# Newest sum first, and the next low weight parts behind the leading narrow products

## The chip, the cores and the metric

One NeuronCore of a Trainium2 chip runs the whole program. The metric is the device time in microseconds of one execution; of the kernel before, three runs were timed.

## The reference, cut to what matters

One decoder block over 256 tokens of width 2048, all in float32:

```python
x = x + 0.5 * swiglu(rms_norm(x, g1), w1_gate, w1_up, w1_down)      # 2048 -> 5632 -> 2048
z = rms_norm(x, gm) @ w_in                                           # 2048 -> 9216
# differential attention of 8 heads on q, k, v; causal depthwise convolution on the GLU part;
# both go through 1024 -> 2048 projections, are gated by sigmoids and added
x = x + merged @ w_out
x = x + 0.5 * swiglu(rms_norm(x, g2), w2_gate, w2_up, w2_down)
return rms_norm(x, final_norm_g)
```

Almost all of the work is matrix products of 256 tokens with weights that are read once from memory.

## The kernel before

**Split products.** Each float32 operand is split into a high part, the value rounded to the fp32r type that TensorE multiplies, and a low part, the remainder. A product is high times high, plus high times low, plus low times high. ScalarE (ACT) makes the high part of a weight block (`wh`, line 94), VectorE (DVE) the low part by subtraction (`wl`, line 103).

**Units and halves.** Weights come in units of 512 rows by 512 columns (1 MB, one DMA on SyncE's queue, three raw buffers). A unit has two halves of two 128-row tiles each; a half is the piece that one line-94 and one line-103 instruction split. There are six buffers for high halves and four for low halves. So the low halves of a unit can be written only when the low products of the unit two before it are done. `Weights.next` (lines 109 to 124) hands out the next half, and before that emits the splits of later halves: high ones up to six halves from the present one, low ones up to four. Behind a low part that ends a raw unit the DMA of a later unit is issued (line 107).

**`lin`** (lines 321 to 369) keeps the weights stationary and makes four PSUM tiles of 128 columns by 512: the left 256 take the high products, the right 256 the products of the low parts of the activations. Per unit there are 16 wide products (line 331, 512 moving columns: both parts of the activations against the high weights) and 16 narrow ones (line 335, 256 moving columns, low weights). Odd units and the last unit of a `lin` run narrow then wide, the others wide then narrow, so that two units' wide products, and two units' narrow ones, stand together. There are 5 PSUM buffers for such tiles, so the next `lin` takes the free one and then those of this `lin` in order. The feed-forward layers call `lin` for gate, up and the first layer's down product; the mixer for the GLU, q and k columns; and `w_out` too. `lin_tok` (lines 379 to 388) is the other form, with activations stationary.

**Carrying off.** In the last unit, after the four wide products of a column tile, that tile's evacuation generator is appended to `flows`; `tick` then takes every flow one stage further, oldest first, and runs side jobs at a given rate. A feed-forward evacuation has as its first stage ACT's copy of the right half of PSUM (line 392), DVE's sum (394) and DVE's product with the gate or the scale (424 or 404). A later stage is ACT's high part of the activation (261) and the next one DVE's low part (263); for a gate it is ACT's Silu (406) and a GpSimd product (407). `residual_evac` has two DVE sums (441, 442). Each engine runs its instructions in the order in which the program emits them.

**Start.** In the first `lin`, `before(u)` splits two tiles of x (lines 256 and 258, ACT and DVE; GpSimd squares them) one half ahead of the products, and `halves` takes the units by halves with `next(early=False)`: the low parts go four halves ahead, the high ones as they are needed.

Of the kernel before, what the change touches and what calls it, by code (L numbers as in the profile page):

```python
# [25 lines left out]
KU = 4  # L26
KH = 2
# [14 lines left out]
class Weights:  # L42
# [54 lines left out]
    def low_to(self, n):  # L97
        while self.nlow < min(n, len(self.units) * KU // KH):
# [6 lines left out]
            if k + KH == KU:  # L105
                del self.raw[u]
                self.load_to(u + 1 + self.raw_bufs)

    def next(self, held=0, early=True):


        i = self.i

        def ahead(bufs):
            n = i + bufs - held
            if self.extra and n > min(self.extra) and i <= max(self.extra):
                n = min(n + len(self.extra), max(self.extra) + 1 + bufs)
            return n

        if early:  # L120
            self.high_to(ahead(self.high_bufs))
        self.low_to(ahead(self.low_bufs))
        self.i += 1
        return self.highs.pop(i), self.lows.pop(i)

# [6 lines left out]
class Side:  # L132
# [8 lines left out]
    def tick(self, n=1):  # L141
        for job in list(self.jobs):
            job[2] += n * job[1]
            while job[2] >= 1:
                job[2] -= 1
                if next(job[0], self) is self:
                    self.jobs.remove(job)
                    break
# [7 lines left out]
def block_kernel(  # L156
# [57 lines left out]
    W = Weights(nc, wpool, units, moving)  # L214
# [97 lines left out]
    flows = []  # L312

    def tick(n=1):

        for f in list(flows):
            if next(f, flows) is flows:
                flows.remove(f)
        side.tick(n)

    def lin(nk, xs, evac, before=None):

        ps = [psum.tile([P, CK], F32, name="ps_mm", tag="mm") for _ in range(4)]
        nu = nk // KU

        def high(ct, parts, kt, i):
            w = parts[i // KH][0][:, i % KH, ct * P:(ct + 1) * P]  # L330
            nc.tensor.matmul(ps[ct], lhsT=w, rhs=xs(kt + i), start=(kt + i == 0), stop=(kt + i == nk - 1))  # L331

        def low(ct, parts, kt, i):
            w = parts[i // KH][1][:, i % KH, ct * P:(ct + 1) * P]
            nc.tensor.matmul(ps[ct][:, T:2 * T], lhsT=w, rhs=xs(kt + i)[:, 0:T], start=False, stop=False)  # L335

        def halves(u):

            for h in range(KU // KH):
                before(u * (KU // KH) + h)  # L340
                parts = [W.next(early=False)]
                for i in range(KH):
                    for ct in range(4):
                        high(ct, parts, u * KU + h * KH, i)
                for ct in range(4):
                    for i in range(KH):
                        low(ct, parts, u * KU + h * KH, i)
                tick(4)

        for u in range(nu):  # L350
            last = u == nu - 1
            if before is not None and not last:
                halves(u)
                continue
            parts = []
            for h in range(KU // KH):
                if before is not None:
                    before(u * (KU // KH) + h)
                parts.append(W.next(held=h))
            for product in ((low, high) if last or u % 2 == 1 else (high, low)):  # L360
                for ct in range(4):
                    for i in range(KU):
                        product(ct, parts, u * KU, i)
                    if product is high:
                        if last:
                            flows.append(evac(ct, ps[ct]))
                        tick(1.4)
                    elif ct % 2 == 1:
                        tick(1.2)
# [28 lines left out]
    def ffn_up(h, rstd, grp, a, before=None, late=None):  # L398
        s_2 = None

        def pair_of(ci, s_t):
# [19 lines left out]
            def up_evac(ct, ps):  # L421
# [4 lines left out]
                yield from split(a(ci * 4 + ct), t)  # L426

            lin(KT, h, gate_evac, before if ci == 0 else None)
            if late is not None and ci == 0:
                side.add(gate_late(), 0.5)  # L430
            lin(KT, h, up_evac)

        for ci in range(len(grp)):
# [14 lines left out]
    def next_norm(h, acc, g):  # L448
        def f(kt):
            yield  # L450
            add_square(acc, xT[:, kt, :], kt == 0)
            yield from split_scaled(h(kt), xT[:, kt, :], g[:, kt:kt + 1])
        return f
# [5 lines left out]
    def split_x(kt):  # L459

        fs = [split_scaled(h1(kt + k), xT[:, kt + k, :], g1_sb[:, kt + k:kt + k + 1]) for k in range(2)]
        for f in fs:
            next(f)
        for f in fs:
            next(f, None)
        for k in range(2):
            add_square(acc1, xT[:, kt + k, :], kt + k == 0, square=nc.gpsimd)

    def start(u):
        if u == 0:  # L470
            W.ahead = 1
            split_x(0)
            W.split_first()
        if u < 7:
            split_x(2 * u + 2)
        else:
            W.ahead = 3

    loads = {}

# [50 lines left out]
    for gi, grp in enumerate(groups):  # L531
        a = split_pair("Q", "a1_")
        if gi == 0:
            ffn_up(h1, rstd1, grp, a, start, rstd_steps(acc1, rstd1, D, 1e-6))
        else:
            ffn_up(h1, rstd1, grp, a)
        last = None
        if gi == len(groups) - 1:
            hm = split_pair("P", "hm_")
            accm, rstdm = norm_tiles("m")  # L540
            last = next_norm(hm, accm, loads["gm"])
        for dc in range(4):
            lin(len(grp) * 4, a, residual_evac(dc, 0.5, last))
# [487 lines left out]
```

## Time and profile before

| what | value |
|---|---|
| median of three runs | 2100.95 us (2100.57 to 2101.76) |
| profiled execution, own time | 2100.18 us |
| its span, first to last instruction | 2098.4 us |
| TensorE busy | 2065.3 us, 98% |
| VectorE busy | 1375.9 us, 66% |
| ScalarE busy | 1004.8 us, 48% |
| GpSimd busy | 190.6 us, 9% |
| mean granted TensorE clock | 0.997 |
| DMA | 189 GB/s over the span |

Busy time of an engine is the union of its instructions. TensorE's weight loads (PEld) overlap its products (PE). A row of the timeline can hold several instructions one after the other (x4), and ends with the idle time of the engine before them and what ended it.

### The profile page before, as it was taken

To read this page: it belongs to the slowest core of one execution; us is meant where nothing else is said; L and a number is where in the kernel's file an instruction comes from. 1 tells how busy PE (TensorE), PEld (TensorE's weight loads), DVE (VectorE), ACT (ScalarE), POOL (GpSimd) and SP (SyncE) were. 2 spreads that over 40 slices of the span, in tenths; PEclk is the share of its full clock that TensorE was granted. 3 is DMA by queue.
4 is the path that set the end of the run, shared out by engine and by line. 5 is a ranking of instruction groups with operands and counts; after the bars stand their busy time and mean duration, and the time that the engine had idled before them with its cause. 6 is when DMAs were issued, how large, how long until landed. Compare 5 with 4: busy or idle time off the path is not lost.

```text
span 2098.4 us, 28546 instructions
## 1 busy us (share of the span) xinstructions
PE 2065.3 (98%) x11230; PEld 1775.8 (85%) x11230; DVE 1375.9 (66%) x1915; ACT 1004.8 (48%) x1456; POOL 190.6 (9%) x227
## 2 busy tenths in 40 slices
PE   7999999999999999999999999999999999999998
PEld 6888888888888888888778888888888888888887
DVE  8565555665565785889888666665655655645565
ACT  6454344443344554445555744554443444434443
POOL 6201012110010110000000000100100001000011
PEclk9999999999999999999999999999999999999999
DMA  6645555566545545555545555554455555554553
GB/s 241 197 171 212 188 177 206 189 216 218 181 180 202 193 174 201 181 187 186 183 166 180 198 181 181 198 203 180 168 214 183 184 195 181 201 193 168 203 198 121
DMA packets 57735, 397.54 MB, mean 189 GB/s; under 512 B 6888, under 2 KB 6992, under 8 KB 10752
## 3 DMA queue, kind: packets, MB, share of 16 engines
q1 hardware_dynamic: 55872, 390.10, 52.2%
q0 software_dynamic: 1728, 5.61, 0.9%
q8 instruction: 88, 1.44, 0.3%
q14 instruction: 47, 0.39, 0.1%
HBM read 392.00 MB, written 3.68 MB: 189 GB/s over the span
## 4 chain that ended last, share of the span: by engine, by line
PE 88%; DVE 7%; ACT 2%; DMA 1%; issue 1%; SPq 0%; DVEq 0%; ACTq 0%
PE ps_mm L331 40%; PE ps_mm L335 21%; PE ps_mm L375 9%; PE ps_mm L376 9%; PE ps_mm L377 9%; DVE wl L103 3%; DVE t L394 2%; DVE t L424 1%; ACT rh L392 1%; DMA w<-in_ffn_w_gate_dram 1%; ACT a L261 1%; DMA w<-in_ffn_w_down_dram 1%; PE ps_s L718 0%; PE ps_o L763 0%; PE ps_tr L907 0%
## 5 line engine op out<-in xcount | busy, mean ns | idle before, releaser
L103 DVE TENSOR_TENSOR wl<-w,wh 128x1024 fp32r<-128x1024 f32 x731 | 883.3, 1248 | 484.2 <-ACT wh L94 239.9
L94 ACT ACTIVATE wh<-w 128x1024 fp32r<-128x1024 f32 x731 | 742.8, 1053 | 704.0 <-PE ps_mm L331 377.5
L331 PE MATMUL ps_mm<-h,wh 128*128 128x512 f32 x2816 | 665.2, 392 | 10.8 <-DVE h L258 10.8
L331 PEld LDWEIGHTS ps_mm<-h,wh 128*128 128x128 f32 x2816 | 523.0, 189 | 117.4 <-ACT wh L84 6.2
L335 PEld LDWEIGHTS ps_mm<-h,wl 128*128 128x128 f32 x2816 | 340.9, 188 | 25.4 <-DVE wl L103 18.1
L335 PE MATMUL ps_mm<-h,wl 128*128 128x256 f32 x2816 | 349.8, 279 | 11.2 <-DVE wl L103 11.2
L407 POOL TENSOR_TENSOR s_t<-s_t,rstd 128x256 f32<-128x256 f32 x88 | 82.7, 940 | 1158.8 <-ACT s_t L406 1158.8
L331 PE MATMUL ps_mm<-a,wh 128*128 128x512 f32 x704 | 164.9, 390 | 0.4 <-DVE t L394 0.4
L331 PEld LDWEIGHTS ps_mm<-a,wh 128*128 128x128 f32 x704 | 130.4, 188 | 26.9 <-DVE t L394 0.8
L392 ACT ACTIVATE rh<-ps_mm 128x256 f32<-128x256 f32 x208 | 77.3, 372 | 153.7 <-PE ps_mm L331 153.7
L375 PE MATMUL ps_mm<-wl,a 128*128 128x512 f32 (+1 forms) x344 | 133.1, 387 | 0.0
L377 PE MATMUL ps_mm<-wh,a 128*128 128x512 f32 (+1 forms) x344 | 132.1, 384 | 0.0
L376 PE MATMUL ps_mm<-wh,a 128*128 128x512 f32 (+1 forms) x344 | 131.9, 384 | 0.0
L375 PE MATMUL ps_mm<-wl,hm 128*128 128x512 f32 x320 | 129.8, 406 | 0.0
L377 PE MATMUL ps_mm<-wh,hm 128*128 128x512 f32 x320 | 125.1, 391 | 0.0
L376 PE MATMUL ps_mm<-wh,hm 128*128 128x512 f32 x320 | 124.9, 390 | 0.0
L331 PE MATMUL ps_mm<-hm,wh 128*128 128x512 f32 x512 | 121.0, 392 | 0.0
L331 PEld LDWEIGHTS ps_mm<-hm,wh 128*128 128x128 f32 x512 | 94.7, 188 | 19.1
L619 DVE SCALAR_TENSOR_TENSOR y_sb<-u_sb,cw_sb,y_sb 128x256 f32<-128x256 f32 x240 | 105.0, 478 | 0.0
L394 DVE TENSOR_TENSOR t<-ps_mm,rh 128x256 f32<-128x256 f32 x112 | 47.5, 424 | 63.1 <-ACT rh L392 62.9
L335 PEld LDWEIGHTS ps_mm<-a,wl 128*128 128x128 f32 x704 | 84.5, 188 | 4.5 <-DVE wl L103 2.7
L335 PE MATMUL ps_mm<-a,wl 128*128 128x256 f32 x704 | 85.6, 278 | 1.9 <-DVE wl L103 1.9
(194 smaller groups left out, 1708.2 us busy)
## 6 DMA issues: line engine op xcount, KB each, us to landing
w<-in_ffn_w_up_dram SPq DMA_DIRECT2D x88, 1024.0 KB, 4.9
w<-in_ffn_w_down_dram SPq DMA_DIRECT2D x88, 1024.0 KB, 4.9
w<-in_ffn_w_gate_dram SPq DMA_DIRECT2D x85, 1024.0 KB, 4.9
w<-in_w_in_dram SPq DMA_DIRECT2D x72, 1024.0 KB, 4.8
w<-in_w_out_dram SPq DMA_DIRECT2D x16, 1024.0 KB, 4.9
w<-in_w_attn_branch_dram SPq DMA_DIRECT2D x8, 1024.0 KB, 4.8
w<-in_w_conv_branch_dram SPq DMA_DIRECT2D x8, 1024.0 KB, 4.8
w<-in_ffn_w_gate_dram SPq DMA_DIRECT2D x5, 512.0 KB, 8.5
```

What stands on the lines that cost most here:

```text
L94: self.nc.scalar.activation(wh, self.raw[u][:, k:k + KH], AF.Copy)
L103: self.nc.vector.tensor_tensor(wl, self.raw[u][:, k:k + KH], self.highs[h].bitcast(F32), ALU.subtract)
L261: nc.scalar.activation(dst[:, 0:T], src, AF.Copy)
L331: nc.tensor.matmul(ps[ct], lhsT=w, rhs=xs(kt + i), start=(kt + i == 0), stop=(kt + i == nk - 1))
L335: nc.tensor.matmul(ps[ct][:, T:2 * T], lhsT=w, rhs=xs(kt + i)[:, 0:T], start=False, stop=False)
L375: nc.tensor.matmul(ps, lhsT=hi, rhs=wl[:, kk, :], start=(first and kk == 0), stop=False)
L376: nc.tensor.matmul(ps, lhsT=hi, rhs=wh[:, kk, :], start=False, stop=False)
L377: nc.tensor.matmul(ps, lhsT=lo, rhs=wh[:, kk, :], start=False, stop=(last and kk == KH - 1))
L392: nc.scalar.activation(r, ps[:, T:2 * T], AF.Copy, scale=scale)
L394: nc.vector.tensor_tensor(dst, ps[:, 0:T], r, ALU.add)
L407: nc.gpsimd.tensor_tensor(s, s, rstd, ALU.mult)
L619: nc.vector.scalar_tensor_tensor(y, src, w, y, ALU.mult, ALU.add)
```

## The change

Four edits. `tick` runs the flows newest first. `Weights.next` makes low parts up to the four-halves limit only where `early` is set; in `halves` it makes them to one half beyond the present one. A new method `more_lows(n)` emits the low parts of n halves more than `next` allows. In a unit whose narrow products lead (odd units, and the last), `more_lows(1)` is called between its narrow and its wide products, and `more_lows(2)` before the third of its four column tiles of wide products. The attribute `W.ahead`, which nothing reads, goes.

```diff
--- before.py
+++ after.py
@@ -106,6 +106,10 @@
                 del self.raw[u]
                 self.load_to(u + 1 + self.raw_bufs)
 
+    def more_lows(self, n):
+
+        self.low_to(self.i + self.low_bufs - KU // KH + n)
+
     def next(self, held=0, early=True):
 
 
@@ -119,7 +123,9 @@
 
         if early:
             self.high_to(ahead(self.high_bufs))
-        self.low_to(ahead(self.low_bufs))
+            self.low_to(ahead(self.low_bufs))
+        else:
+            self.low_to(i + 2)
         self.i += 1
         return self.highs.pop(i), self.lows.pop(i)
 
@@ -313,7 +319,8 @@
 
     def tick(n=1):
 
-        for f in list(flows):
+
+        for f in flows[::-1]:
             if next(f, flows) is flows:
                 flows.remove(f)
         side.tick(n)
@@ -357,8 +364,13 @@
                 if before is not None:
                     before(u * (KU // KH) + h)
                 parts.append(W.next(held=h))
-            for product in ((low, high) if last or u % 2 == 1 else (high, low)):
+            order = (low, high) if last or u % 2 == 1 else (high, low)
+            for product in order:
+                if product is high and order[0] is low:
+                    W.more_lows(1)
                 for ct in range(4):
+                    if product is high and order[0] is low and ct == 2:
+                        W.more_lows(2)
                     for i in range(KU):
                         product(ct, parts, u * KU, i)
                     if product is high:
@@ -468,13 +480,10 @@
 
     def start(u):
         if u == 0:
-            W.ahead = 1
             split_x(0)
             W.split_first()
         if u < 7:
             split_x(2 * u + 2)
-        else:
-            W.ahead = 3
 
     loads = {}
 
```

## Rows read from the trace of the kernel before

**Rows 1.** Page, part 1: busy us per engine, share of the span, instructions.

```profile
PE 2065.3 (98%) x11230; PEld 1775.8 (85%) x11230; DVE 1375.9 (66%) x1915; ACT 1004.8 (48%) x1456; POOL 190.6 (9%) x227
```

**Rows 2.** Waits of TensorE: who for whom, us in total, times, longest.

```profile
PE ps_mm L335 <- DVE wl L103: 13.9, 41, 0.6
PE ps_mm L331 <- DVE h L258: 10.8, 4, 5.8
...
PEld ps_mm L335 <- DVE wl L103: 22.0, 41, 0.8
```

**Rows 3.** Chain of waits in time order: start us, us, what.

```profile
68.34 7.28 PE ps_mm L331 x32
...
113.33 7.28 PE ps_mm L331 x32
...
225.28 7.28 PE ps_mm L331 x32
...
269.02 7.28 PE ps_mm L331 x32
```

**Rows 4.** Timeline, 56 to 92 us: start, us, engine, line, idle before.

```profile
57.55 0.38 ACT L392 ACTIVATE rh<-ps_mm 128x256 f32<-128x256 f32 x1 [2.14 <-PE ps_mm L331]
...
59.35 0.37 ACT L392 ACTIVATE rh<-ps_mm 128x256 f32<-128x256 f32 x1
...
62.77 0.36 ACT L392 ACTIVATE rh<-ps_mm 128x256 f32<-128x256 f32 x1
...
64.04 2.35 DVE L103 TENSOR_TENSOR wl<-w,wh 128x1024 fp32r<-128x1024 f32 x2
...
66.45 1.90 PE L335 MATMUL ps_mm<-h,wl 128*128 128x256 f32 x14 [0.51 <-DVE wl L103]
...
77.33 2.36 DVE L103 TENSOR_TENSOR wl<-w,wh 128x1024 fp32r<-128x1024 f32 x2 [5.73 <-ACT wh L94]
...
79.11 7.44 PE L331 MATMUL ps_mm<-h,wh 128*128 128x512 f32 x32
...
80.66 0.42 DVE L394 TENSOR_TENSOR s_t<-ps_mm,rh 128x256 f32<-128x256 f32 x1 [0.97 <-ACT rh L392]
```

**Rows 5.** Groups: line, engine, operation, shapes, count, busy us, mean ns, idle.

```profile
L394 DVE TENSOR_TENSOR s_t<-ps_mm,rh 128x256 f32<-128x256 f32 x88 | 37.3, 424 | 70.1 <-ACT rh L392 70.1
...
L442 DVE SCALAR_TENSOR_TENSOR xT<-ps_mm,xT 128x256 f32<-128x256 f32 x64 | 27.2, 424 | 2.2
...
L407 POOL TENSOR_TENSOR s_t<-s_t,rstd 128x256 f32<-128x256 f32 x88 | 82.7, 940 | 1158.8 <-ACT s_t L406 1158.8
```

**Rows 6.** Timeline of the start, 10 to 38 us.

```profile
13.19 1.28 DVE L103 TENSOR_TENSOR wl<-w,wh 128x1024 fp32r<-128x1024 f32 x1 [1.79 <-ACT wh L94]
...
15.04 1.78 DVE L103 TENSOR_TENSOR wl<-w,wh 128x1024 fp32r<-128x1024 f32 x1 [0.57 <-ACT wh L94]
...
16.75 1.69 DVE L258 SCALAR_TENSOR_TENSOR h<-xT,g_sb,h 128x256 fp32r<-128x256 f32 x2
...
17.63 3.78 PE L331 MATMUL ps_mm<-h,wh 128*128 128x512 f32 x8 [4.46 <-DVE h L258]
...
31.38 1.63 DVE L103 TENSOR_TENSOR wl<-w,wh 128x1024 fp32r<-128x1024 f32 x1
...
32.93 1.71 DVE L258 SCALAR_TENSOR_TENSOR h<-xT,g_sb,h 128x256 fp32r<-128x256 f32 x2
...
37.97 0.38 ACT L392 ACTIVATE rh<-ps_mm 128x256 f32<-128x256 f32 x1 [0.52 <-PE ps_mm L331]
```

**Rows 7.** Timeline around 460 us, a late weight block.

```profile
459.91 2.01 ACT L94 ACTIVATE wh<-w 128x1024 fp32r<-128x1024 f32 x2 [6.23 <-DMA w<-in_ffn_w_down_dram]
...
466.12 1.20 PE L331 MATMUL ps_mm<-a,wh 128*128 128x512 f32 x4 [0.38 <-DVE t L394]
```

**Rows 8.** Busy us per engine, clock and DMA in two 50 us windows.

```profile
1450.00:1500.00 50.00, 48.88 (x287) 42.81 (x286) 31.87 (x43) 23.29 (x35) 3.71 (x4) 1.00 0.51 185
...
1550.00:1600.00 50.00, 50.00 (x222) 41.16 (x220) 24.91 (x23) 19.67 (x19) 0.00 (x0) 1.00 0.56 197
```

## The prediction

> **What bounds the kernel now.** I read the page's busy times first. TensorE is busy 2065.3 of 2098.4 us [rows 1], so whatever the change does to the other engines counts only through some 33 us in which TensorE stands still, and through what its weight loads lose beside that. The list of waits says what ends these: 41 times the low part of a weight half (line 103), with 13.9 us of idle product time and 22.0 us of idle weight loading; and four waits on VectorE's split of x, 10.8 us in all, at the very start [rows 2].
>
> What one of the 41 costs in full is read from the chain. From the wide products at 225.28 to those at 269.02 lie eight units without such a wait: 43.74 us. From 68.34 to 113.33 lie also eight units (two linears of the gate and up columns) with two waits: 44.99 us [rows 3]. That is 0.63 us for each wait: idle time, the lost prefetch of weights and the refilling of the pipeline.
>
> The timeline shows why [rows 4]. The wait at 66.45 is in the narrow products of the second unit of a linear, and it is for the second of two low parts that VectorE began at 64.04 and made in 2.35 us. Their buffers had been free since the last unit's narrow products ended, about 1.1 us before the first copy at 57.55 (0.91 us of wide products for that tile, and 0.2 us to the copy). VectorE came so late because the program puts these two behind the four evacuations of the last unit. And these are slow: ScalarE's copies for line 392 start at 57.55, 59.35 and, the fourth, 62.77, some 1.7 us apart, while the wide products end a column tile each 0.91 us (32 of them take 7.28 us [rows 3], four to a tile). With the oldest flow first, ScalarE's next copy stands behind the older tile's split, which itself waits for VectorE's product.
>
> **Part 1, the low parts ahead of the evacuations.** I lay the new order over the linear whose wide products start at 79.11 [rows 4]. VectorE makes the next unit's pair from 77.33 to 79.69, as now. The first moved half follows to 80.87 (1.18 us, half of 2.35); its buffer came free at 79.11. The first sum, now at 80.66, starts at 80.87. A tile takes two operations of 0.42 us, with the step between them 0.9 us [rows 5]: first tile to 81.8, second to 82.7. Then the second moved half, to 83.9. The third tile's sum has read PSUM by 84.3.
>
> Two things must hold. The moved halves are needed at 79.11 + 3.64 (wide) + 3.64 (next unit, wide) + 1.83 (its narrow ones, 43.74 / 8 less 3.64) = 88.2: they are 4.3 us early, and the wait goes whole. And the next linear starts at 82.75, its fourth tile at 85.48, in the buffer that the third tile of this linear leaves at 84.3: 1.2 us to spare. `residual_evac` reads PSUM with both of its sums (0.42 us each [rows 5]), so 0.45 us later: 0.7 us to spare. In the mixer a convolution step or two stand between; I count on some margin there too. So I cost the move at nothing: the next linear's first three tiles cover it. If that cover were gone, each us of delay would be a us of TensorE.
>
> What is queued behind the new wait: the first moved half waits for the narrow products just emitted. Behind it on VectorE are the sums of tiles whose wide products come later still on TensorE, and side jobs; nothing that TensorE needs before. In odd units that are not the last there is no evacuation behind it. The moved half also frees the raw buffer earlier, so SyncE issues the next 1 MB load earlier; its queue then carries only these loads, in the same order. ScalarE's high parts are emitted six halves ahead already and don't move.
>
> Gain: 41 waits by 0.63 us, 25.6 us. From below it is bounded by the idle product time alone, 13.9 us [rows 2], if the rest were something else; I take 25.6, since the stretches differ by nothing but these waits. What is late next in these stretches: nothing that I can name; elsewhere eight-unit stretches run without a gap, and TensorE's clock is granted in full both with gaps and without (1.00 at 48.88 and at 50.00 busy of 50 us [rows 8]).
>
> **Part 2, newest flow first.** The count and length of instructions stay. A tile's sum is no longer behind an older tile's split, so sums follow the products at 0.91 us. The older stage (activation split, Silu, GpSimd product) comes one copy later, 0.4 us; its reader is a linear away, except for the last tiles before a down product, which are needed only in its last unit. Alone this would also make the low parts some 2 us earlier, so parts 1 and 2 remove the same wait twice and are counted once. One stop of its own goes: at 459.91 a weight block lands late, ScalarE stands for 6.23 us with the copies behind it, and at 466.12 a fourth tile waits for a sum, 0.38 us [rows 7]. With earlier loads and quicker sums I count 0.4 us, between 0 and 0.6.
>
> **Part 3, the start.** Now VectorE makes three low parts in a row, with 1.79 and 0.57 us of waiting for weights, and only then, at 16.75, the low part of x that TensorE waits for until 17.63, for 4.46 us [rows 6]. With low parts only one half ahead that split of x comes right behind the first of them, at some 11.4, and TensorE goes on at about 13.2, when the next weight half is ready, if x has landed. But from there VectorE is the bound: a pair of x splits (1.69 us) and a low part (1.63) take 3.3 us a half, TensorE's products 2.7. What counts is when the last unit, whose narrow products lead, has both low parts. Now all that VectorE does up to its last x split ends at 32.93 + 1.71 = 34.64. The change leaves one low part (1.63 at 31.38) for after that and fills up to 2.36 us of waiting: 30.7 to 31.3. Narrow and wide products (1.83 + 3.64) then end at 36.2 to 36.8; now they end 0.2 us before ScalarE's fourth copy, at 37.8 [rows 6]. I take 0.9 us of gain, from the later of the two. It could be 4.4 (the whole stop, if TensorE were the bound) or a loss of 1.4 (if none of VectorE's waiting is filled).
>
> The sum: 25.6 + 0.4 + 0.9 = 26.9 us from the profiled execution's own 2100.18: 2073.3. That execution was 0.8 us below the median of the three runs, so 2074.1 for a median.
>
> [...] The trace has GpSimd's products with a mean of 0.94 us, in the gate linears, beside the evacuations [rows 5], and low parts of 1.63 us in the start, where GpSimd works all the time, against 1.18 later [rows 4, 6]. [...]
>
> **The rivals.**
>
> *Half of it.* Something I don't see keeps the second moved half late, say the high half or the raw block behind which it stands. For: the waits on VectorE are for the second half of a pair. Against: high parts are two units ahead. Half of 25.6 is lost: 2087. Chance 0.06.
>
> *Blocked.* [...] Chance 0.05.
>
> *Evacuation becomes the bound, slower.* If a low part in these stretches comes to 1.63 us, the four ahead of the third sum (the pair, the first moved half, the second) push it to 84.3 + 4 x 0.45 = 86.1, and in `residual_evac` to 86.5, against 85.48. With 0.1 us to refill that is 0.7 us in each of 44 gate and up linears and 1.1 us in some 20 others: 53 us lost, 27 gained, 2127. Stops begin at a low part of 1.5 us, and from about 1.55 they outweigh the gain. Against: pairs of 2.35 us in the very stretches [rows 4]. Chance 0.04.
>
> *It doesn't do what it says*: the moved low parts wait for the same instant as before, because a low buffer is not free at 79.11. Then the order of the sums alone changes: 2100. Against: the buffer count, four, and the narrow products that end there. Chance 0.03.
>
> **How the numbers follow.** The forecast has 0.82. Its own bounds: at best 2100.18 - 25.6 - 4.4 - 0.6 + 0.8 = 2070, at worst 2100.18 - 13.9 + 1.4 + 0.8 = 2088. The range 2069 to 2087 holds nearly all of it and the edge of "half": some 0.85. A difference below 0.2%, 4.2 us, can't be told from none. Faster: forecast, half and blocked, 0.93. Same: 0.03. Slower: 0.04.
>
> **What would show it.** Right: no waits, or next to none, of line 335 on line 103; eight gate and up units in 43.7 us; VectorE's sums 0.9 us apart; in the last unit a line-103 instruction between the end of its narrow products and the first sum. At the start the stop near 17.63 gone, smaller stops later on x or low parts, and the fourth copy at 36 to 37.5. Wrong: stops of line 331 on sums (394, 442), or waits of line 335 still there at the second unit of a linear.

## The result, and the profile after

| | before | changed | ratio, 95% interval |
|---|---|---|---|
| median | 2101.34 us | 2072.3 us | 0.9862 [0.9845, 0.988] |
| range of runs | 2100.57 to 2101.76 | 2071.92 to 2072.87 | |
| span of the profiled execution | 2098.4 us | 2070.7 us | |

The forecast was 2074.1 us, in a range of 2069 to 2087. The change gains 29.0 us between the medians (27.7 between the profiled spans); 26.9 were forecast. That the totals agree so closely is in part luck: one term came out larger and another with the other sign, as the account below shows.

TensorE's row of the page, beside [rows 1]: the same products, 13.9 us less of busy time, in a span 27.7 us shorter. So about half of the gain is idle time that is gone, and half is products that took less time; the trace does not divide these further.

```profile
PE 2051.4 (99%) x11230; PEld 1771.1 (86%) x11230; DVE 1364.6 (66%) x1915; ACT 1017.2 (49%) x1456; POOL 202.1 (10%) x227
```

The list of waits, beside [rows 2] (who waited for whom, us in total, times, longest). None of the 41 waits for a low part is left: they all came after the start, and the four in the list now are new ones, all in the first 31 us. No stop on a sum has come in their place. The 6.0 us are the time until the first product; in the kernel before they are the 5.8 among the waits for x:

```profile
PE ps_mm L338 <- ACT wh L84: 6.0, 1, 6.0
PE ps_mm L342 <- DVE wl L103: 5.2, 4, 2.7
```

The chain of waits in time order, beside [rows 3]: wide products of eight units of gate and up columns. They take 43.74 us, what such units took without a wait before, where two waits made it 44.99.

```profile
68.37 7.28 PE ps_mm L338 x32
...
112.11 7.28 PE ps_mm L338 x32
```

The timeline of an up linear and the next gate linear, beside [rows 4]:

```profile
58.41 0.38 ACT L404 ACTIVATE rh<-ps_mm 128x256 f32<-128x256 f32 x1 [2.12 <-PE ps_mm L338]
...
59.32 0.38 ACT L404 ACTIVATE rh<-ps_mm 128x256 f32<-128x256 f32 x1 [0.53 <-PE ps_mm L338]
...
60.22 0.38 ACT L404 ACTIVATE rh<-ps_mm 128x256 f32<-128x256 f32 x1
...
60.64 1.22 DVE L103 TENSOR_TENSOR wl<-w,wh 128x1024 fp32r<-128x1024 f32 x1
...
61.19 0.39 ACT L404 ACTIVATE rh<-ps_mm 128x256 f32<-128x256 f32 x1
...
64.56 3.82 PE L342 MATMUL ps_mm<-h,wl 128*128 128x256 f32 x32
...
77.36 3.50 DVE L103 TENSOR_TENSOR wl<-w,wh 128x1024 fp32r<-128x1024 f32 x3 [6.36 <-ACT wh L94]
...
79.14 7.44 PE L338 MATMUL ps_mm<-h,wh 128*128 128x512 f32 x32
...
80.78 0.42 DVE L406 TENSOR_TENSOR s_t<-ps_mm,rh 128x256 f32<-128x256 f32 x1
...
82.40 1.76 DVE L103 TENSOR_TENSOR wl<-w,wh 128x1024 fp32r<-128x1024 f32 x1
...
84.09 0.41 DVE L406 TENSOR_TENSOR s_t<-ps_mm,rh 128x256 f32<-128x256 f32 x1
```

ScalarE's four copies now stand 0.9 us apart (58.41, 59.32, 60.22, 61.19), where they stood 1.7 apart. The first moved low part is the third of the three at 77.36; the first sum follows at 80.78, where the forecast had 80.87; the second moved part stands at 60.64 or 82.40, between the second and the third sum. The third sum ends at 84.5 (forecast 84.3), 1.0 us before the next linear's fourth tile needs its buffer (79.14 + 3.64 + 2.73 = 85.5). In the `w_out` linear whose wide products start at 1288.89 the same margin is 0.65 us (forecast 0.7), and in the mixer's linear at 779.96, to which the forecast gave no number, it is only 0.3 us. The narrow products at 64.56 run through 32 without a gap.

The start, beside [rows 6]:

```profile
11.14 1.72 DVE L264 SCALAR_TENSOR_TENSOR h<-xT,g_sb,h 128x256 fp32r<-128x256 f32 x2
...
13.18 2.08 PE L338 MATMUL ps_mm<-h,wh 128*128 128x512 f32 x8
...
27.46 1.69 DVE L264 SCALAR_TENSOR_TENSOR h<-xT,g_sb,h 128x256 fp32r<-128x256 f32 x2
27.59 0.50 PE L342 MATMUL ps_mm<-h,wl 128*128 128x256 f32 x2 [2.08 <-DVE wl L103]
...
29.08 6.53 DVE L103 TENSOR_TENSOR wl<-w,wh 128x1024 fp32r<-128x1024 f32 x4
...
30.76 3.36 PE L342 MATMUL ps_mm<-h,wl 128*128 128x256 f32 x14 [2.67 <-DVE wl L103]
33.92 6.68 PE L338 MATMUL ps_mm<-h,wh 128*128 128x512 f32 x24
...
38.82 0.38 ACT L404 ACTIVATE rh<-ps_mm 128x256 f32<-128x256 f32 x1 [0.52 <-PE ps_mm L338]
```

The stop near 17.63 is gone: the split of x stands at 11.14 and products go on at 13.18. But two stops have come before the last unit, 2.08 and 2.67 us, both for its low parts, and the fourth copy is at 38.82, 0.85 us later than before. The windows say why the last unit's products were slow, 14 narrow ones taking 3.36 us (columns: stretch, then busy us of TensorE, weight loads, VectorE, ScalarE and GpSimd with their counts, then granted clock, DMA share, GB/s):

```profile
28.00:30.00 2.00, 0.10 (x1) 0.00 (x0) 2.00 (x3) 0.87 (x1) 1.84 (x4) 0.83 0.17 70
30.00:32.00 2.00, 1.24 (x6) 1.24 (x7) 2.00 (x2) 1.13 (x2) 2.00 (x2) 0.50 0.35 57
32.00:34.00 2.00, 2.00 (x11) 2.00 (x11) 2.00 (x3) 0.00 (x0) 1.92 (x2) 0.50 0.79 319
34.00:36.00 2.00, 2.00 (x6) 1.57 (x6) 1.60 (x1) 0.14 (x1) 2.00 (x2) 0.50 0.79 250
```

Behind the stops the granted clock was 0.50, from about 29.3 to 36.1. Before, the only such stretch at the start lay behind the old stop:

```profile
14.00:18.00 4.00, 0.37 (x1) 0.37 (x2) 3.43 (x4) 3.92 (x7) 3.84 (x4) 0.74 1.04 425
18.00:22.00 4.00, 4.00 (x12) 3.23 (x12) 4.00 (x5) 2.03 (x4) 3.84 (x5) 0.50 1.01 428
```

### The profile page after: what moved, and what is told of

Its sections match the earlier page's. It is cut to its first block, busy times and chain, and to the rows that moved or that the text cites. A ratio compares the mean times of both kernels' runs of the same rounds, so it can differ in the third digit from the quotient of the medians.

```text
span 2070.7 us, 28562 instructions
## 1 busy us (share of the span) xinstructions
PE 2051.4 (99%) x11230; PEld 1771.1 (86%) x11230; DVE 1364.6 (66%) x1915; ACT 1017.2 (49%) x1456; POOL 202.1 (10%) x227
## 4 chain that ended last, share of the span: by engine, by line
PE 98%; DVE 0%; ACT 0%; ACTq 0%; issue 0%
PE ps_mm L338 47%; PE ps_mm L342 24%; PE ps_mm L387 9%; PE ps_mm L388 9%; PE ps_mm L389 9%; PE ps_s L727 0%; PE ps_o L772 0%; PE ps_mg L880 0%; PE ps_tr L916 0%; PE ps_at L762 0%; PE ps_mean L302 0%; PE ps_tr L815 0%; ACT sqf L976 0%; DVE x L974 0%; ACT x L995 0%; ACTq L1036 0%
## 5 line engine op out<-in xcount | busy, mean ns | idle before, releaser
L342 PE MATMUL ps_mm<-h,wl 128*128 128x256 f32 x2816 | 340.0, 278 | 5.2 <-DVE wl L103 5.2
L419 POOL TENSOR_TENSOR s_t<-s_t,rstd 128x256 f32<-128x256 f32 x88 | 89.3, 1024 | 1124.9 <-ACT s_t L418 1124.9
L389 PEld LDWEIGHTS ps_mm<-wh,a 128*128 128x128 f32 x344 | 64.5, 188 | 13.9
```

The source lines that it names most:

```text
L389: nc.tensor.matmul(ps, lhsT=lo, rhs=wh[:, kk, :], start=False, stop=(last and kk == KH - 1))
L419: nc.gpsimd.tensor_tensor(s, s, rstd, ALU.mult)
```

## The experiments

Ratios are to the kernel before, run on the same chip.

**Each part by itself.** First the moved low parts alone, in the start as before and with flows oldest first:

```diff
-        for f in flows[::-1]:
+        for f in list(flows):
...
-            self.low_to(ahead(self.low_bufs))
-        else:
-            self.low_to(i + 2)
+        self.low_to(ahead(self.low_bufs))
```

> The moved low parts alone; flows oldest first and the start as in the kernel before. Theory: each of the two order changes removes the 41 waits by itself. Then no wait of line 335 on line 103 stays, the steady part gains the 28.6 us that the changed kernel gained behind its start, and the start costs nothing: about 2072 us (2071 to 2074). Rival: the moved low parts alone push the third sum, whose copies are still 1.7 us apart, past the start of the next linear's fourth tile: stops of the wide products on sums, 2076 to 2095.

Measured: 2074.61 us, 0.9877 [0.9863, 0.989]. No wait of a narrow product on a low part is left in it, so the moved parts do remove all 41 by themselves. The time lies between the theory (up to 2074) and its rival (from 2076): it stays 2.6 us above the same kernel with newest flow first (2071.97, below), by the rival's mechanism. The timeline of a `w_out` linear shows it: oldest first, VectorE makes the second moved part (1.71 us) and then an older tile's split (line 262) before the third tile's sums, which end at 1295.42, and the next linear's fourth tile stops:

```profile
1292.04 1.71 DVE L103 TENSOR_TENSOR wl<-w,wh 128x1024 fp32r<-128x1024 f32 x1
1293.68 0.96 DVE L262 SCALAR_TENSOR_TENSOR h<-xT,g_sb,h 128x256 fp32r<-128x256 f32 x1
...
1295.00 0.42 DVE L452 SCALAR_TENSOR_TENSOR xT<-ps_mm,xT 128x256 f32<-128x256 f32 x1
...
1295.58 1.16 PE L336 MATMUL ps_mm<-mg,wh 128*128 128x512 f32 x4 [0.22 <-DVE xT L452]
```

There are three such stops, and the linears behind them fall back by 1.5 us in all against the kernel with newest flow first. The list of waits of the weight loads has five more, for first-stage sums (line 404):

```profile
PEld ps_mm L336 <- DVE t L404: 1.7, 5, 0.4
```

At these five, one of them in the up linear at 63.20, TensorE falls back by another 1.0 us in all. So nearly the whole difference is sums that came too late in the oldest-first order.

Then newest flow first alone, on the kernel before:

```diff
-        for f in list(flows):
+        for f in flows[::-1]:
```

> Newest flow first alone. Theory: copies 0.91 us apart, the fourth sum about 2 us earlier, so the pair of low parts that stands behind it is ready some 1 us before it is needed: the 41 waits go, about 2072 us (2071 to 2075). Rival: the low parts are still behind all evacuations and stay late in the linears with the longest ones: half of the waits stay, 2086; or all, 2101.

Measured: 2072.13 us, 0.9864 [0.985, 0.9877]: the whole gain from one line. The pair of low parts still stands behind all evacuations, but these are done sooner; the pair that began at 64.04 in [rows 4] begins at 62.90, though this linear is 0.7 us later (its first copy at 58.26 against 57.55), and is ready at 65.25, before the second unit's narrow products (the second half of the 32 at 64.41):

```profile
58.26 0.38 ACT L392 ACTIVATE rh<-ps_mm 128x256 f32<-128x256 f32 x1 [2.13 <-PE ps_mm L331]
...
59.17 0.38 ACT L392 ACTIVATE rh<-ps_mm 128x256 f32<-128x256 f32 x1 [0.53 <-PE ps_mm L331]
...
61.04 0.38 ACT L392 ACTIVATE rh<-ps_mm 128x256 f32<-128x256 f32 x1
...
62.90 2.35 DVE L103 TENSOR_TENSOR wl<-w,wh 128x1024 fp32r<-128x1024 f32 x2
...
64.41 3.82 PE L335 MATMUL ps_mm<-h,wl 128*128 128x256 f32 x32
```

So the two order changes remove the same waits twice, as part 2 of the prediction had it. With newest flow first in place, the moved low parts neither cost nor gain anything that can be measured: 2072.13 us without them, 2071.97 with them and the old start (next).

**The start.** Parts 1 and 2 with the start as before, and the new start alone:

```diff
-            self.low_to(ahead(self.low_bufs))
-        else:
-            self.low_to(i + 2)
+        self.low_to(ahead(self.low_bufs))
```

> The changed kernel with the low parts of the start four halves ahead as before. Theory: the new start costs 0.85 us (the second linear begins at 38.62 instead of 37.77), so 2071.5 us, 0.5 to 1.2 us below the changed kernel, second linear at 37.8. Rival: the loss in the start is given back later or was chance: 2072.3.

```diff
-        self.low_to(ahead(self.low_bufs))
+        if early:
+            self.low_to(ahead(self.low_bufs))
+        else:
+            self.low_to(i + 2)
```

> The new start alone on the kernel before. Theory: 0.85 us slower, about 2102.2 us; second linear at 38.6, and TensorE's clock granted at 0.50 behind its stop at 28 to 31 us. Rival (the prediction's own step): 0.9 us faster, 2100.4.

Measured: 2071.97 us, 0.9863 [0.9848, 0.9878], for the first, 0.3 us below the changed kernel; 2101.11 us, 1.0004 [0.9995, 1.0012], for the second, no change that can be told from none. Both medians lean towards a loss, of 0.3 and 0.8 us, but neither the theory's loss of 0.85 us nor the prediction's gain of 0.9 can be told from nothing: the new start moves the time by no more than starts differ by themselves. The product that sums the squares of x (line 296 before the change) stands at the same place of TensorE's queue in all these kernels, behind the first linear and two tiles of the second. With the old start it began at 39.59, 39.91, 40.29 and 40.29 in four profiles, with the new one at 40.44, 39.84, 39.96, 40.19 and 40.49 in five. The row of the kernel with the old start kept, and that of the new start alone:

```profile
40.29 0.59 PE L300 MATMUL ps_mean<-acc,ones 128*128 128x256 f32 x2
39.84 0.59 PE L299 MATMUL ps_mean<-acc,ones 128*128 128x256 f32 x2
```

The stop is the same in the new start alone: it waits from 28.1 for a low part until 30.80, and the clock from 28 to 34 is 0.50.

**A better start.** If VectorE bounds the start, the last unit's two low parts should stand ahead of the last x splits. First ahead of the last pair, then ahead of the last two:

```diff
-            self.low_to(i + 2)
+            self.low_to(i + (3 if i == 5 else 2))
```

> The changed kernel, but in the sixth half of the start both low parts that the last unit's leading narrow products need stand ahead of the last x split. Theory: VectorE bounds the start, and the changed kernel stops at 27.59 to 30.76 for the low part behind that split; now it is ready at about 29.1, the narrow products end 1.6 us earlier, and if the stop is short enough that the clock stays granted in full the second linear begins at 34.6 to 37.0 instead of 38.6: 2069 to 2071 us. Rival: starts differ by chance as much (37.8 to 38.6 in five profiles so far) and nothing is seen in the time: 2072.

```diff
-            self.low_to(i + 2)
+            self.low_to(i + (4 if i == 4 else 2))
```

> The changed kernel, but in the fifth half of the start three low parts are made, so that the last unit's two stand ahead of its last two pairs of x splits. Theory: VectorE's work is the same, the low parts are ready at about 27.4, so TensorE's stop before the last unit shrinks to under 2 us and its clock stays granted in full; the wide products then wait for the x splits until 30.8 and end at about 33.8: second linear at 33.8 to 35, 2068 to 2070 us. Rival as for the other start: 2072.

Measured: 2071.3 us, 0.9863 [0.985, 0.9876], and 2073.52 us, 0.9872 [0.9859, 0.9886]. The first keeps a stop of 2.0 and one of 1.0 us and its clock falls as well, to 0.50 from 28 to 34 us; its second linear begins 1.2 us earlier. Its median is 1.0 us lower, but so was the kernel before on that chip (2100.09 against 2101.34 us), and the ratio is that of the changed kernel: no gain is shown, as its rival had it. The second misses its forecast of 2068 to 2070, though it does all that was expected up to the end of the first linear: stops of 0.55 and 1.08 us before the last unit, the clock at 1.00 from 28 to 36 us, the second linear at 33.91, 4.7 us earlier. Then it gives all of it back:

```profile
35.59 0.74 DVE L406 TENSOR_TENSOR s_t<-ps_mm,rh 128x256 f32<-128x256 f32 x2
36.05 1.21 PE L338 MATMUL ps_mm<-h,wh 128*128 128x512 f32 x4 [1.08 <-DVE s_t L406]
...
39.35 1.13 PE L302 MATMUL ps_mean<-acc,ones 128*128 128x256 f32 x2 [2.09 <-POOL acc L281]
...
40.00:42.00 2.00, 2.00 (x7) 1.54 (x6) 0.99 (x2) 0.42 (x1) 0.00 (x0) 0.50 1.00 422
```

Sums stand behind three low parts (1.08 us of stop), and the product that sums the squares waits 2.09 us for GpSimd, which adds up x until 39.3. That product stands in TensorE's queue ahead of all further weights' products. Behind these stops the granted clock falls after all: it is 0.50 from 40 to 42 us (the last row, a window with the columns as above). The third linear begins at 61.56, 0.6 us later than in the changed kernel. So one more kernel with that start, the product queued later:

```diff
-            self.low_to(i + 2)
+            self.low_to(i + (4 if i == 4 else 2))
...
-                side.add(gate_late(), 0.5)
+                side.add(gate_late(), 0.5, delay=8)
```

> The start with the last unit's low parts first (second linear at 33.91), and the product that sums the squares of x queued 8 ticks later on TensorE, since there it waited until 39.35 for GpSimd's sum. Theory: GpSimd's sum was what ended last in the start; with the product behind it the 4.7 us won before are kept but for one stop on a sum (1.1 us) and what the clock loses: third linear at 57 to 58.5 instead of 60.93, 2069 to 2070.5 us. Rival: the gate's scaling, which hangs on that product, comes late for the up sums or the low parts of the second linear come late, and the gain goes there: 2072.

Measured: 2070.08 us, 0.9853 [0.9836, 0.9869], the fastest of all, 2.2 us below the changed kernel, and within its forecast. The kernel with both moved parts at once (below), whose median is within 0.2 us of the changed kernel's, ran on the same chip: 2071.92 to 2072.67 us there, 2069.56 to 2070.40 here, with no overlap. The product no longer waits, and the clock stays at 1.00 from 28 to 44 us:

```profile
36.60 3.45 PE L338 MATMUL ps_mm<-h,wh 128*128 128x512 f32 x12 [0.97 <-DVE s_t L406]
...
43.68 0.59 PE L302 MATMUL ps_mean<-acc,ones 128*128 128x256 f32 x2
```

Its third linear begins at 58.69, not at 58.5 or earlier: the next high parts came 0.6 us late, and a weight load waited 0.55 us for another sum. That is 2.2 us earlier than in the changed kernel (60.93), as much as the whole difference in time. In this start, then, time was lost in a chain of three: first to low parts, then to sums behind low parts, then to GpSimd.

**The cover.** The prediction costed the two low parts ahead of the third sum at nothing, with 1.2 us to spare. To see that this is where the limit is, the second one was made twice, then three times, in the last unit of each linear:

```diff
...
-            self.nc.vector.tensor_tensor(wl, self.raw[u][:, k:k + KH], self.highs[h].bitcast(F32), ALU.subtract)
+            for _ in range(self.times):
+                self.nc.vector.tensor_tensor(wl, self.raw[u][:, k:k + KH], self.highs[h].bitcast(F32), ALU.subtract)
...
-                        W.more_lows(2)
+                        W.times = 2 if last else 1        # then 3
+                        W.more_lows(2)
+                        W.times = 1
```

> The changed kernel, with the second moved low part of each linear's last unit made twice (the same values written again): 1.2 us more of VectorE ahead of the third sum in 68 linears. Theory of the cover: in the changed kernel's gate linears the third sum is read by 84.5 and needed at 85.5, in the up linears by 62.2 and 63.65, in linears with residual sums with 0.7 us to spare. So 22 gate linears stop for 0.35 us and some 16 others for 0.6 us, the up linears don't: 18 us more, 2090 (2080 to 2098), and the stops are wide products that wait for a sum. Rival: VectorE has slack there that I don't see, 2072.

> The same with the low part made three times, 2.4 us more. Theory of the cover: now all kinds of linears stop: gate 1.55, up 1.1, residual 1.8, mixer about 1 us: 95 us more than the changed kernel, 2167 (2140 to 2185); behind the cover each us of VectorE is about a us of TensorE. Rival: the stops of one linear take from those of the next, and it grows by less than half of that: under 2120.

Measured: 2103.04 us, 1.0013 [1.0004, 1.0022], and 2195.75 us, 1.0455 [1.0441, 1.0469]: 31 and 123 us over the changed kernel, where 18 and 95 were expected; both lie above their ranges. The stops are the ones expected, wide products that wait for a sum, and once the cover is gone the second copy costs three times the first. The size of the first was missed mainly because in a gate linear a low part stands beside GpSimd's product and takes 1.7 us, not 1.2:

```profile
81.95 2.57 POOL L423 TENSOR_TENSOR s_t<-s_t,rstd 128x256 f32<-128x256 f32 x2 [24.16 <-ACT s_t L422]
82.17 3.44 DVE L105 TENSOR_TENSOR wl<-w,wh 128x1024 fp32r<-128x1024 f32 x2
...
85.53 0.41 DVE L410 TENSOR_TENSOR s_t<-ps_mm,rh 128x256 f32<-128x256 f32 x1
...
85.99 1.19 PE L340 MATMUL ps_mm<-h,wh 128*128 128x512 f32 x4 [0.55 <-DVE s_t L410]
```

Two low parts in 3.44 us; the third sum starts at 85.53, the fourth tile at 85.99 instead of 85.3, 0.7 us late. The four units from 68.14 to 90.84 take 22.70 us where they took 21.87 (half of 43.74): 0.83 for a gate linear, where 0.35 were expected. Over 22 gate linears that is, by estimate, some 11 of the 13 us that were missed. The waits by what they are for, two rows of the kernel with the part made twice (19 on gate sums, longest 0.7) and one of that with it made three times:

```profile
PE ps_mm L340 <- DVE s_t L410: 10.6, 19, 0.7
...
PE ps_mm L340 <- DVE xT L458: 5.4, 7, 1.1
...
PE ps_mm L340 <- DVE s_t L410: 37.4, 21, 2.0
```

Not all of the 123 us is waiting. The mean granted clock of that kernel is 0.989, against 0.997, and its four runs are ordered by it, from 2190.97 us at 0.993 to 2199.93 at 0.988. By that slope (8.96 us for 0.005), an estimate, some 14 us are the clock.

Last, both moved parts ahead of the first sum:

```diff
-                    W.more_lows(1)
+                    W.more_lows(2)
...
-                    if product is high and order[0] is low and ct == 2:
-                        W.more_lows(2)
```

> The changed kernel with both moved low parts ahead of all four tiles of wide products, so the first sum comes 1.2 us later and the third at the same time. Theory: what counts is the third sum, so nothing changes: 2072 us, no stops on sums. Rival: the first two sums are late for the next linear's second and third tile, 2080.

Measured: 2072.16 us, 0.9864 [0.9849, 0.9879], and no stop on a sum in its list of waits. Whether the second one stands ahead of the first sum or of the third makes no difference.

## Why the prediction was right, and where it was not

*What bounds the kernel.* Right. The 41 waits were nearly all that was won, and their reason was the one read from [rows 4]: low parts behind evacuations that were themselves slowed by the oldest-first order. Either order change alone removes the waits.

*Part 1, cost and margin.* Right to 0.2 us in the gate linear, though by two errors that nearly cancel: the second moved part began at 82.40 instead of 82.7, and took 1.76 us instead of 1.18. That the move costs nothing is shown by the kernels with and without it under newest flow first; what limits it was shown with the cover taken away: the third sum decides, and one low part more is enough to lose the whole gain.

*Part 1, the gain.* The term was 25.6 us, and with the 0.4 of part 2 the forecast behind the start was 26.0. There the profiled spans differ by 27.7 + 0.85 = 28.6 us. So 2.6 us too little here stand against 1.75 too much in the start (0.9 of gain forecast, 0.85 of loss in the profile), and the sum is off by only 0.8. The price of one wait was read from one stretch with 0.63 us; the next two linears show 0.67 (their wide products start at 158.40 after 113.33 [rows 3], 45.07 us for 43.74). And the stretch with the late weight block, counted at 0.4 us beside its waits, cost 2.8 us in all: of the kernel before, eight units from 436.96 to 483.53 are 46.57 us. In the changed kernel the same stretch shows no loss (440.11 to 483.84, 43.73 us).

```profile
436.96 7.28 PE ps_mm L331 x32
...
483.53 7.28 PE ps_mm L331 x32
```

*Part 2.* Right, and stronger than put: alone it takes all of the gain, since it makes the low parts 1.85 us earlier against the linear's first copy (some 2 us were forecast). Together with part 1 the two are counted once, as they were. Where it does more than part 1 is with older tiles' later stages, in the residual linears above all, which it moves behind the third sum: 2.6 us.

*Part 3.* The step that failed. The stop at 17.63 went, VectorE became the bound, and both low parts of the last unit were ready at 30.7, where 30.7 to 31.3 was forecast. But from there 5.5 us were counted for its products. In the profile they took from 30.76 to about 38.6, 7.8 us: TensorE had stood for most of 5 us, and its clock was granted at 0.50 for the first 5.3 of them. At 1.00 the same 14 narrow products took 1.86 us (27.64, in the better start), here 3.36. The prediction had taken the clock to be full with gaps and without, from windows with gaps of well under 1 us [rows 4, 8]; that does not carry over to the stops of 2.08 and 2.67 us here or to the 4.46 us of the old start, behind which it was 0.50. The gain of 0.9 us became 0.85 us of loss in this profile, and nothing that can be measured in the runs of the two kernels that differ in the start alone; the forecast's own bounds (4.4 of gain to 1.4 of loss) held it, the lower one by luck, since it was set for a VectorE that fills none of its waiting and not for the clock. What had been left out was what the old start showed too: its stop had its own 0.50 stretch.

*The rivals.* "Half of it" and "it doesn't do what it says" did not come: no wait for a low part is left outside the start. "Blocked", a moved low part that stands behind a whole GpSimd product of 0.94 us, did not come either; no run shows that term in a gate linear, and what the runs show in its place is smaller. A moved low part took 1.76 us in a gate linear (82.40) and 1.22 in an up linear (60.64), and GpSimd's products rose to a mean of 1.02 us from 0.94 [rows 5]:

```profile
82.19 2.57 POOL L419 TENSOR_TENSOR s_t<-s_t,rstd 128x256 f32<-128x256 f32 x2 [23.75 <-ACT s_t L418]
...
87.78 0.74 POOL L419 TENSOR_TENSOR s_t<-s_t,rstd 128x256 f32<-128x256 f32 x1 [1.34 <-ACT s_t L418]
...
L419 POOL TENSOR_TENSOR s_t<-s_t,rstd 128x256 f32<-128x256 f32 x88 | 89.3, 1024 | 1124.9 <-ACT s_t L418 1124.9
```

The rows show what such a low part is longer by. The one at 82.40 began 0.21 us after a GpSimd product; a product that began while no low part ran took 0.74 us (87.78), so 0.53 us of it were left, by estimate, and the low part took 0.54 more. In the start of the same trace one that began 0.50 us after a GpSimd product took only 1.37 us (13.16), and one that began 0.72 us after, 1.23 (10.00). Where the low part came first (49.33) it took 1.22, and GpSimd's product (49.94) took 1.21 instead of 0.74. So in these four cases the one that began second took longer, by 0.01 to 0.54 us. But for one of 4.66 us beside a GpSimd instruction of 6.34 us (1980.58), no low part of the trace took over 1.77 us, 0.55 more than the 1.22, and the margin of 1.0 us held. "Evacuation becomes the bound" did not come; what it would cost is seen in the kernel with one low part more: 2103 us, slower than before.

## What to carry to other kernels

When an in-order engine both empties accumulators and prepares the next operands, look at which of its instructions wait for something recent, and let the newest accumulator's first stage go ahead of older tiles' later stages: one line did here what four edits did. Before moving work ahead of an evacuation, compute when the accumulator's buffer is needed again, and take the moved instruction's time from a row where the neighbours are busy as they will be there. Where a stop at the start is removed, follow what waits next all the way to the next stage, the granted clock included.

## What the runs showed of the hardware

A long stop of TensorE at the start cost more than its own length. In the changed kernel TensorE made two narrow products between 25.5 and 30.76 us, and then ran at a granted clock of 0.50 until about 36.1: by estimate, from the 14 narrow products that took 3.36 us there and 1.86 at 1.00, some 2.4 of these 5.3 us came on top of the stops. After stops of 0.55 and 1.08 us with products between them (the better start) it stayed at 1.00. What brings the clock down is not shown. The length of one stop does not settle it: in the kernel with the low part made three times a stop of 1.81 us that ended at 137.83 was followed by a clock of 0.50 from 138 to 140 us, and one of 1.81 us that ended at 186.51 by 1.00 throughout.

And the same start, run in several kernels, reached the same product at 39.59 to 40.29 us, so 0.7 us in one profile's start says nothing by itself.
